# A two-layer transformer block in split fp32: sevens for a second group of k-tiles in half of the gate and up blocks

## The chip, the cores and the metric

One core of one Trainium2 chip. The metric is the device time of one execution in microseconds. Three runs of the kernel before took 2272.69, 2273.01 and 2273.35 us (median 2273.01).

## The reference

The input is one sequence of 256 positions with 2048 features, and two layers. Each layer adds a mixer (gated delta rule and gated linear recurrence in layer 0, two kinds of attention in layer 1) and then a feed-forward part of width 5632:

```python
def swiglu(hn, w_gate, w_up, w_down):
    return (jax.nn.silu(hn @ w_gate) * (hn @ w_up)) @ w_down
...
        h = h + swiglu(rmsnorm(h, ffn_norm[layer]), ffn_w_gate[layer], ffn_w_up[layer], ffn_w_down[layer])
    return rmsnorm(h, final_norm)
```

Everything is fp32. Only the feed-forward parts are changed here.

## The kernel before

**Split products.** TensorE multiplies in the type fp32r. Each fp32 number is taken as a high part (a cast to fp32r, on ACT) and a low part (the number less its high part, on DVE), and a product is the sum of three: high by high, high by low, low by high. `load` (L161) draws a weight tile of 128 x 1024 (512 KB) into a raw buffer, through SP's queue; `split` (L171) makes its parts `whi` (L174, ACT) and `wlo` (L175, DVE). Raw buffers: three in a pool, and in the feed-forward part a fourth, `raw4`, for each fourth load. High parts have four buffers, low parts three.

**The feed-forward part** (`ffn`, L444) runs over 11 columns of 512 hidden features (b = 0 to 10), in pieces of 4, 4 and 3. For each column one block computes gate and up: the four results are F[t][i], t for the two halves of the positions, i for gate or up. Then, per piece, two blocks (p = 0, 1) multiply the hidden features with the down weights, and add to h. The activations (`X` or `hid`) are the stationary operand, 128 x 128; the weights stream, 512 columns for each matmul.

**A block** (`block`, L371) has 16 units of weights (12 in the down blocks of the last piece): a unit is two k-tiles of one of the two weight matrices. Four units, that is four k-tiles of both, form a group m. A plain unit is one load, one cast, one subtraction and 12 matmuls (two halves t, two k-tiles, three products). The group m = 0 is done by sevens instead (Strassen's method in Winograd's form, on the 2 x 2 of halves of positions and k-tiles, and of k-tiles and matrices): 7 products of 6 matmuls in place of 8. It needs sums of weights (`total`, L334: an addition on DVE into T, a cast `thi` on ACT, a subtraction `tlo` on DVE), T1 to T4, and combinations of the activations, made once for a whole layer (X) or piece (hid) by `combine` (L344). Its seven steps, with the loads that they draw:

| step | load | into |
|---|---|---|
| 1 | b11 | M0, b11 itself |
| 2 | b12 | M1, T1 = b11 + b12 |
| 3 | b22 | F01, b22 itself |
| 4 | | M3, T3 = b12 + b22 |
| 5 | | M2, T2 = T1 + b22 |
| 6 | b21 | F00, b21 itself |
| 7 | | F10, T4 = T2 + b21 |

(In the kernel the signs are in the combinations and in the last sums.) After the last step `ends` (L411) makes four sums e of the M banks (one copy on ACT, four steps on DVE), and at the block's end F and e are added.

**The order of the work.** The program writes the units in order, and between the plain units the steps by sevens: step k is written behind plain unit j as soon as k < (j - lead + 2) x steps / gaps (L437). With 12 plain units, lead 2 and trail 3, gaps is 7, so one step follows each of the plain units 1 to 7 (counted from 0), and four plain units stand behind the last one. In the first block of a layer the lead is 5 and the gaps 4: seven steps within four plain units. The framework then schedules each engine's queue, which stays in that order on the chip; a tile waits until one of its tag's buffers is free.

**Hooks** are written ahead of a plain unit: `turn` (L449, twice, ahead of units 2 and 3) transposes the block before's result `fa` on TensorE into a bank Ph and writes its parts into `hid`; `combine` of X in the first block, of the first four hid tiles in the second block of a piece. PSUM has eight banks: four for F, and four that M and Ph share.

Of the kernel before, what the change touches and what calls it, by code (L numbers as in the profile page):

```python
# [4 lines left out]
F32, F32R, I32 = dt.float32, dt.float32r, dt.int32  # L5
# [6 lines left out]
T = 256  # L12
# [35 lines left out]
def body(tc, A, out):  # L48
# [9 lines left out]
    wh = pool("wh", 4)  # L58
    wl = pool("wl", 3)
    acc = pool("acc", 4, space=PSUM)  # L60
    msp = pool("msp", 4, space=PSUM)
    mx, ogp = Phase(), Phase()
    loads, more = [0], []
# [16 lines left out]
    X = res.tile([128, NK, 2, T], F32R, name="X", tag="X")  # L80
# [88 lines left out]
        return raw  # L169

    def split(raw):  # L171
        hi = wh.tile([128, 1024], F32R, name="whi")
        lo = wl.tile([128, 1024], F32R, name="wlo")
        S.copy(hi, raw)  # L174
        V.tensor_sub(lo, raw, hi.bitcast(F32))  # L175
        return hi, lo
# [100 lines left out]

    def sumsq(g, *ts):
        for t in ts or range(2):
            j = mx.tile([128, 512], F32, name="junk", tag="t2", bufs=4)  # L280
            S.activation(j, h[:, t, g * 512:(g + 1) * 512], AF.Square, accum_out=ssp[:, t, g:g + 1])

    def to_x(g, w, late=False):
# [59 lines left out]

    def combine(x4):  # L344

        f = mx.tile([128, 4, T], F32, name="cf", tag="cf", bufs=1)
        c = mx.tile([128, 4, 2, 128], F32, name="cc4", tag="cc4", bufs=1)
        r = mx.tile([128, 2, 4, 2, 128], F32R, name="comb", tag="comb", bufs=2)
        V.tensor_tensor(out=f, in0=x4[:, :, 0].bitcast(F32), in1=x4[:, :, 1].bitcast(F32), op=ALU.add)
        a11, a21, a12, a22 = (f[:, 2 * j:2 * j + 2, t * 128:(t + 1) * 128] for j in range(2) for t in range(2))  # L350
        for i, (x, y) in enumerate(((a21, a22), (a21, a11), (a22, c[:, 1]), (a12, c[:, 2]))):
            V.tensor_tensor(out=c[:, i], in0=x, in1=y, op=ALU.subtract)
        S.copy(r[:, 0], c)
        V.tensor_tensor(out=r[:, 1], in0=c, in1=r[:, 0].bitcast(F32), op=ALU.subtract)
        return r
# [15 lines left out]
    def block(src, x, comb, nd, hooks, tail=0, lead=2):  # L371

        plain = [(i, u) for m in range(nd) if m not in comb for u in (2 * m, 2 * m + 1) for i in range(2)]
        n, ns = len(plain) // 2, len(comb)
        F = [[Bank(acc.tile([128, 512], F32, name=f"F{t}{i}", tag="acc"), n + (ns if t * i == 0 else 0)) for i in range(2)]
             for t in range(2)]  # L380
        M = [Bank(ms([128, 512], f"M{j}"), ns) for j in range(4)]

        def xs(k, t):
            return [x(k)[:, j, t * 128:(t + 1) * 128] for j in range(2)]

        def seven(m):
            c = comb[m]()
            cx = lambda i: lambda kk: [c[:, j, i, kk] for j in range(2)]
            q = lambda j, t: lambda kk: xs(4 * m + 2 * j + kk, t)
            b11 = load(src(0, 2 * m))  # L390
            M[0].add(q(0, 0), split(b11))
            yield
            b12 = load(src(1, 2 * m))
            t, w = total(b11, b12, "T1")
            M[1].add(cx(0), w)
            yield
            b22 = load(src(1, 2 * m + 1))
            F[0][1].add(cx(3), split(b22))
            yield
            M[3].add(cx(1), total(b12, b22, "T3")[1])  # L400
            yield
            t, w = total(t, b22, "T2")
            M[2].add(cx(2), w)
            yield
            b21 = load(src(0, 2 * m + 1))
            F[0][0].add(q(1, 0), split(b21))
            yield
            F[1][0].add(q(1, 1), total(t, b21, "T4")[1])
            yield

        def ends():  # L411
            c1, v, w5, w7 = (mx.tile([128, 512], F32, name=f"e{i}", tag=f"e{i}", bufs=1) for i in range(4))
            S.copy(c1, M[0].t)
            for o, a, b, op in ((v, M[2], c1, ALU.subtract), (w5, M[1], v, ALU.add), (v, M[3], v, ALU.add), (w7, M[3], w5, ALU.add)):
                V.tensor_tensor(out=o, in0=a.t, in1=b, op=op)
            return [[c1, w5], [v, w7]]

        sevens = [s for m in comb for s in [seven(m)] for _ in range(7)]
        trail = 3 if nd > 3 else 2
        gaps = max(len(plain) - lead - trail, 1)  # L420
        held, e, k = [], None, 0
        for j, (i, u) in enumerate(plain):
            if j in hooks:
                hooks[j]()
            w = unit(src(i, u))
            held.append((i, u, w))
            if j < len(plain) - tail:
                todo, held = [(*held[0], (0, 1))], []
            elif j < len(plain) - 1:
                continue  # L430
            else:
                todo = [(*y, (t,)) for t in range(2) for y in held]
            for i1, u1, w1, tt in todo:
                for t in tt:
                    F[t][i1].add(lambda kk: xs(2 * u1 + kk, t), w1)
            tick()
            while k < len(sevens) and k < (j - lead + 2) * len(sevens) // gaps:  # L437
                next(sevens[k])
                k += 1
                if k == len(sevens):  # L440
                    e = ends()
        return [[y.t for y in f] for f in F], e

    def ffn(L, then, fin=None):  # L444

        gu, dn = A[f"gu{L}"], A[f"dn{L}"]
        todo, cx, ch = [], {}, {}

        def turn():  # L449
            hid, j, t, a = todo.pop(0)  # L450
            P = ms([128, 4, 128], "Ph")
            for i in range(4):
                PE.transpose(P[:, i], a[:, i * 128:(i + 1) * 128], tb["ident"])  # L453
            d = hid[:, 4 * j:4 * j + 4, :, t * 128:(t + 1) * 128]
            S.copy(d[:, :, 0], P)
            V.tensor_tensor(out=d[:, :, 1], in0=P, in1=d[:, :, 0].bitcast(F32), op=ALU.subtract)

        b = 0
        for piece in (4, 4, 3):
            hid = ogp.tile([128, 16, 2, T], F32R, name="hid", tag="hid")  # L460
            for j in range(piece):
                hooks = {2: turn, 3: turn} if todo else {}
                if b == 0:
                    hooks[4] = lambda: cx.update({0: combine(X[:, 0:4])})
                    hooks[8] = rstd
                if j == 1:
                    hooks[5] = lambda: ch.update({0: combine(hid[:, 0:4])})
                F, e = block(lambda i, u: gu[b, u, i], lambda k: X[:, k], {0: lambda: cx[0]}, 4, hooks, lead=2 if b else 5)
                a = [mx.tile([128, 512], F32, name=f"fa{t}", tag="fa", bufs=4) for t in range(2)]
                for t in range(2):  # L470
                    r = nrm["rs"][:, t:t + 1]
                    V.tensor_tensor(out=a[t], in0=F[t][0], in1=e[t][0], op=(ALU.add, ALU.subtract)[t])
                    S.activation(a[t], a[t], AF.Silu, scale=r)
                for t in range(2):
                    r = nrm["rs"][:, t:t + 1]
                    V.tensor_tensor(out=e[t][1], in0=F[t][1], in1=e[t][1], op=ALU.add)
                    V.scalar_tensor_tensor(out=a[t], in0=e[t][1], scalar=r, in1=a[t], op0=ALU.mult, op1=ALU.mult)
                    todo.append((hid, j, t, a[t]))
                b += 1
            u0 = 2 * (b - piece)  # L480
            for p in range(2):
                end = b == NB and p == 1
                F, e = block(lambda i, u: dn[2 * p + i, u0 + u], lambda k: hid[:, k], {0: lambda: ch[0]}, piece,
                             {2: turn, 3: turn} if todo else {}, 3 if end and fin else 0)
                hs = [[h[:, t, (2 * p + i) * 512:(2 * p + i + 1) * 512] for i in range(2)] for t in range(2)]
                for t in range(2):
                    for i in range(2):
                        V.tensor_tensor(out=e[t][i], in0=hs[t][i], in1=e[t][i], op=ALU.subtract if t > i else ALU.add)
                for t in range(2):
                    for i in range(2):  # L490
                        V.tensor_tensor(out=hs[t][i], in0=F[t][i], in1=e[t][i], op=ALU.add)
                    if end and fin:
                        fin(t)
                if b == NB and not (end and fin):
                    then(2 * p)
                    then(2 * p + 1)
# [674 lines left out]
```

## Time and profile before

| what | value |
|---|---|
| median of three runs | 2273.01 us |
| the profiled execution: its own time | 2272.64 us |
| its span, first to last instruction | 2270.7 us |
| clock granted to TensorE | 0.999 |
| loads of gate and up weights | 352, 512 KB each, median 4.2 us from issue to landing |
| loads of down weights | 176, 512 KB each, 4.1 us |
| read from HBM | 418.22 MB, 185 GB/s over the span |
| low parts (L175) | 744, 1.22 us each |
| high parts (L174) | 744, 1.05 us each |
| sums T (L337) | 136, 1.22 us each |

A row of a group names the line, the engine, the step, what it writes and reads, the count, then the busy time in us, the mean of one in ns, and the idle time of the engine ahead of them with what ended it. A row in order of time has the start, the length, the engine, and in brackets how long its engine had been idle and who released it. A row of waits has the total, the number and the longest. Line numbers are those of the kernel before.

### The profile page before, as it was taken

The numbers are of one execution on the slowest core, as the hardware profiler recorded it, in microseconds if no ns is written. First come the engines' busy times: TensorE is split into PE (matmuls) and PEld (weight loads), VectorE is DVE, ScalarE is ACT, GpSimd is POOL, SyncE is SP. The second block draws the span as 40 slices with busy tenths as digits, with TensorE's granted clock in tenths as the row PEclk, the third lists the DMA queues.
The fourth block names the chain that finished last, engine by engine and source line by source line (L and its number), as shares of the span: only waits on it lengthen the run. The fifth ranks groups of instructions, "written<-read, shape, count | busy, mean of one in ns | idle before, by whom it ended". The sixth has DMA issues, their size and how long they took to land.

```text
span 2270.7 us, 31138 instructions
## 1 busy us (share of the span) xinstructions
PE 2252.9 (99%) x11610; PEld 1901.3 (84%) x11610; DVE 1804.5 (79%) x2655; ACT 1201.8 (53%) x1579; POOL 2.0 (0%) x6
## 2 busy tenths in 40 slices
PE   9999999999999999999999999999999999999998
PEld 8999888878888888888878888888888888888886
DVE  7898676697887887887976658858888888887888
ACT  6765654564554554454644444445554454554554
POOL 0000000000000000000000000000000000000000
PEclk9999999999999999999999999999999999999999
DMA  7444445566666666666555455555666566566564
GB/s 256 151 160 155 140 158 184 179 203 196 194 205 193 195 202 189 200 197 197 191 163 169 153 169 168 166 187 188 195 208 193 190 201 202 184 203 207 183 217 148
DMA packets 118647, 422.35 MB, mean 186 GB/s; under 512 B 13248, under 2 KB 14784, under 8 KB 118368
## 3 DMA queue, kind: packets, MB, share of 16 engines
q1 hardware_dynamic: 118208, 419.84, 58.3%
q8 instruction: 91, 1.49, 0.3%
q14 instruction: 60, 0.49, 0.1%
q10 hardware_dynamic: 288, 0.52, 0.1%
HBM read 418.22 MB, written 2.10 MB: 185 GB/s over the span
## 4 chain that ended last, share of the span: by engine, by line
PE 94%; DVE 2%; DMA 2%; ACT 0%; issue 0%; SPq 0%; DVEq 0%; ACTq 0%
PE F L366 17%; PE F L368 17%; PE F L367 17%; PE Pw L194 7%; PE Pw L199 6%; PE Px L268 5%; PE Px L270 4%; PE Px L269 4%; PE M L367 2%; PE M L368 2%; PE M L366 2%; PE Pw L197 2%; PE Pw L198 2%; DMA raw<-in_gu 1%; PE Ph L453 1%; DVE wlo L175 1%
## 5 line engine op out<-in xcount | busy, mean ns | idle before, releaser
L174 ACT CAST whi<-raw 128x1024 fp32r<-128x1024 f32 x744 | 779.9, 1052 | 899.9 <-PE F L368 375.5
L175 DVE TENSOR_TENSOR wlo<-raw,whi 128x1024 fp32r<-128x1024 f32 x744 | 904.7, 1220 | 324.3 <-PE F L367 122.1
L366 PE MATMUL F<-whi,X 128*128 128x512 f32 x1100 | 431.0, 392 | 0.0
L367 PE MATMUL F<-wlo,X 128*128 128x512 f32 x1100 | 428.4, 389 | 0.0
L368 PE MATMUL F<-whi,X 128*128 128x512 f32 x1100 | 428.1, 389 | 0.0
L199 PE MATMUL Pw<-X,wlo 128*128 128x256 f32 x1104 | 310.5, 281 | 1.1 <-DVE wlo L175 1.1
L368 PEld LDWEIGHTS F<-whi,X 128*128 128x128 f32 x1100 | 206.5, 188 | 43.1
L367 PEld LDWEIGHTS F<-wlo,X 128*128 128x128 f32 x1100 | 206.6, 188 | 42.1 <-DVE wlo L175 0.5
L366 PEld LDWEIGHTS F<-whi,X 128*128 128x128 f32 x1100 | 206.5, 188 | 41.8
L194 PE MATMUL Pw<-X,whi 128*128 128x512 f32 x640 | 230.3, 403 | 0.0
L199 PEld LDWEIGHTS Pw<-X,wlo 128*128 128x128 f32 x1104 | 209.5, 190 | 1.7 <-DVE wlo L175 1.5
L366 PE MATMUL F<-whi,hid 128*128 128x512 f32 x536 | 209.8, 392 | 0.0
L367 PE MATMUL F<-wlo,hid 128*128 128x512 f32 x536 | 208.7, 389 | 0.0
L368 PE MATMUL F<-whi,hid 128*128 128x512 f32 x536 | 208.7, 389 | 0.0
L341 DVE TENSOR_TENSOR tlo<-T,thi 128x1024 fp32r<-128x1024 f32 x136 | 165.7, 1219 | 24.0 <-ACT thi L340 24.0
L340 ACT CAST thi<-T 128x1024 fp32r<-128x1024 f32 x136 | 142.8, 1050 | 38.0 <-DVE T L337 34.9
L194 PEld LDWEIGHTS Pw<-X,whi 128*128 128x128 f32 x640 | 120.2, 188 | 29.4 <-issue 0.7
L197 PE MATMUL Pw<-X,whi 128*128 128x256 f32 x464 | 135.2, 291 | 0.6 <-ACT whi L174 0.6
L198 PE MATMUL Pw<-X,whi 128*128 128x256 f32 x464 | 131.2, 283 | 0.0
L368 PEld LDWEIGHTS F<-whi,hid 128*128 128x128 f32 x536 | 100.6, 188 | 21.0
L367 PEld LDWEIGHTS F<-wlo,hid 128*128 128x128 f32 x536 | 100.7, 188 | 20.8 <-DVE wlo L175 0.3
L366 PEld LDWEIGHTS F<-whi,hid 128*128 128x128 f32 x536 | 100.6, 188 | 20.3
(371 smaller groups left out, 3229.8 us busy)
## 6 DMA issues: line engine op xcount, KB each, us to landing
raw<-in_gu SPq DMA_DIRECT2D x352, 512.0 KB, 4.2
raw<-in_dn SPq DMA_DIRECT2D x176, 512.0 KB, 4.1
raw<-in_w0w SPq DMA_DIRECT2D x74, 512.0 KB, 3.7
raw<-in_wo SPq DMA_DIRECT2D x64, 512.0 KB, 3.6
raw<-in_w1w SPq DMA_DIRECT2D x64, 512.0 KB, 3.6
raw<-in_w1x SPq DMA_DIRECT2D x32, 512.0 KB, 3.6
raw<-in_w0x SPq DMA_DIRECT2D x16, 512.0 KB, 3.5
raw<-in_w0w SPq DMA_DIRECT2D x12, 256.0 KB, 4.6
```

The costliest lines, as they stand in the source:

```text
L174: S.copy(hi, raw)
L175: V.tensor_sub(lo, raw, hi.bitcast(F32))
L194: PE.matmul(P.rearrange("p a b -> p (a b)"), hi[:, kk], X[:, k].rearrange("p a b -> p (a b)"), start=k == 0, stop=False)
L197: PE.matmul(P[:, 0], hi[:, kk], X[:, k, 0], start=k == 0, stop=False)
L198: PE.matmul(P[:, 0], hi[:, kk], X[:, k, 1], start=False, stop=False)
L199: PE.matmul(P[:, 0], lo[:, kk], X[:, k, 0], start=False, stop=k == NK - 1)
L268: PE.matmul(Ps[t], x[:, 0, ts], hi[:, kk], start=k == 0, stop=False)
L340: S.copy(hi, t)
L341: V.tensor_sub(lo, t, hi.bitcast(F32))
L366: PE.matmul(self.t, xh, hi[:, kk], start=self.i == kk == 0, stop=False)
L367: PE.matmul(self.t, xh, lo[:, kk], start=False, stop=False)
L368: PE.matmul(self.t, xl, hi[:, kk], start=False, stop=kk == 1 and self.i == self.n - 1)
```

## The change

- In every second gate and up block (b = 2, 4, 6, 8, 10 of both layers) the group m = 1 is done by sevens as well: 8 plain units, 14 steps. Each group draws its seven steps from its own generator, first all of m = 0, then all of m = 1. The M banks take both groups. The trail there is 2, so gaps is 4, and the 14 steps stand behind plain units 1 (three), 2 (four), 3 (three) and 4 (four); three plain units follow.
- The combination of X for m = 1 is made in block b = 1, ahead of plain unit 8. That of hid moves from the second to the fourth block of a piece of four. `combine` has three result buffers, and takes its two others from the three buffers of T.
- In the feed-forward part each fifth load's high part, and the low part of each load whose number leaves 2 when divided by 4, gets a buffer of its own.
- `junk` and `fa` have two buffers instead of four.

```diff
     def split(raw):
-        hi = wh.tile([128, 1024], F32R, name="whi")
-        lo = wl.tile([128, 1024], F32R, name="wlo")
+        k = loads[0] if more else 0
+        hi = mx.tile([128, 1024], F32R, name="whi", tag="hi5", bufs=1) if k > 0 and k % 5 == 0 else wh.tile([128, 1024], F32R, name="whi")
+        lo = mx.tile([128, 1024], F32R, name="wlo", tag="lo4", bufs=1) if k > 0 and k % 4 == 2 else wl.tile([128, 1024], F32R, name="wlo")
...
-            j = mx.tile([128, 512], F32, name="junk", tag="t2", bufs=4)
+            j = mx.tile([128, 512], F32, name="junk", tag="t2", bufs=2 if more else 4)
...
-        f = mx.tile([128, 4, T], F32, name="cf", tag="cf", bufs=1)
-        c = mx.tile([128, 4, 2, 128], F32, name="cc4", tag="cc4", bufs=1)
-        r = mx.tile([128, 2, 4, 2, 128], F32R, name="comb", tag="comb", bufs=2)
+        f = mx.tile([128, 4, T], F32, name="cf", tag="T", bufs=3)
+        c = mx.tile([128, 4, 2, 128], F32, name="cc4", tag="T", bufs=3)
+        r = mx.tile([128, 2, 4, 2, 128], F32R, name="comb", tag="comb", bufs=3)
...
-        sevens = [s for m in comb for s in [seven(m)] for _ in range(7)]
-        trail = 3 if nd > 3 else 2
+        two = [seven(m) for m in comb]
+        sevens = [two[i] for i in ((0,) * 7 if ns == 1 else (0,) * 7 + (1,) * 7)]
+        trail = 3 if ns == 1 and nd > 3 else 2
...
-                if j == 1:
+                if j == (3 if piece == 4 else 1):
                     hooks[5] = lambda: ch.update({0: combine(hid[:, 0:4])})
-                F, e = block(lambda i, u: gu[b, u, i], lambda k: X[:, k], {0: lambda: cx[0]}, 4, hooks, lead=2 if b else 5)
-                a = [mx.tile([128, 512], F32, name=f"fa{t}", tag="fa", bufs=4) for t in range(2)]
+                if b == 1:
+                    hooks[8] = lambda: cx.update({1: combine(X[:, 4:8])})
+                F, e = block(lambda i, u: gu[b, u, i], lambda k: X[:, k],
+                             {m: lambda m=m: cx[m] for m in range(2 - b % 2 if b else 1)}, 4, hooks, lead=2 if b else 5)
+                a = [mx.tile([128, 512], F32, name=f"fa{t}", tag="fa", bufs=2) for t in range(2)]
```

## The prediction

> **What bounds the kernel now.** I read the page's first part, then the waits of TensorE, then a feed-forward block in order of time. All microseconds are of one profiled execution: its time is 2272.64, its span 2270.7, so 1.94 lie around the span.
>
> ```profile
> span 2270.7 us, 31138 instructions
> PE 2252.9 (99%) x11610; PEld 1901.3 (84%) x11610; DVE 1804.5 (79%) x2655; ACT 1201.8 (53%) x1579; POOL 2.0 (0%) x6
> ```
> ```profile
> PE Pz L90 <- ACT wz L87: 2.3, 1, 2.3
> PE M L367 <- DVE tlo L341: 1.7, 4, 0.5
> PE Pw L199 <- DVE wlo L175: 1.1, 2, 0.8
> PE Prb L311 <- PE Pw L199: 0.8, 1, 0.8
> PE Pw L197 <- ACT whi L174: 0.6, 1, 0.6
> ```
> TensorE is busy 99% and all its listed waits add to 6.5 us. VectorE (DVE) waits for TensorE, not the other way. So time goes with the number of matmuls, as long as nothing else becomes late. The price of one, from the first and the last of 79 matmuls in a row:
>
> ```profile
> 595.78 0.39 PE L368 MATMUL F<-whi,X 128*128 128x512 f32 x1
> ...
> 613.47 0.39 PE L368 MATMUL F<-whi,X 128*128 128x512 f32 x1
> ```
> 17.69 / 78 = 0.2268 us from start to start. (The 0.39 is the pipelined length of one.) A gate and up block with one group by sevens has 186 such matmuls; its length is the distance of the same step in two neighbouring blocks, 566.73 - 523.65 = 43.08 us:
>
> ```profile
> 523.65 0.69 DVE L472 TENSOR_TENSOR fa<-F,e 128x512 f32<-128x512 f32 x1 [0.31 <-PE F L368]
> ...
> 566.73 0.69 DVE L472 TENSOR_TENSOR fa<-F,e 128x512 f32<-128x512 f32 x1 [0.31 <-PE F L368]
> ```
> 186 x 0.2268 = 42.18; the other 0.90 are the two turns (transposes of fa), 0.45 each. VectorE in this block:
>
> ```profile
> 527.70:570.20 42.50, 42.50 (x193) 35.19 (x193) 34.14 (x35) 22.16 (x24) 0.00 (x0) 1.00 0.62 195
> ```
> The columns are length, PE, PEld, DVE, ACT, POOL, clock, DMA share, GB/s. DVE works 34.1 of 42.5 us, ACT 22.2, the clock is full. Its steps:
>
> ```profile
> 531.37 1.22 DVE L175 TENSOR_TENSOR wlo<-raw,whi 128x1024 fp32r<-128x1024 f32 x1
> 532.51 1.22 DVE L341 TENSOR_TENSOR tlo<-T,thi 128x1024 fp32r<-128x1024 f32 x1
> 533.64 1.21 DVE L175 TENSOR_TENSOR wlo<-raw,whi 128x1024 fp32r<-128x1024 f32 x1
> ...
> 548.82 1.23 DVE L341 TENSOR_TENSOR tlo<-T,thi 128x1024 fp32r<-128x1024 f32 x1 [0.85 <-ACT thi L340]
> ...
> 551.77 2.74 DVE L415 TENSOR_TENSOR e<-M,e 128x512 f32<-128x512 f32 x4 [0.36 <-PE M L368]
> ```
> ```profile
> 558.37 0.39 PE L366 MATMUL F<-thi,X 128*128 128x512 f32 x1
> ```
> A step of 1024 columns comes every 1.14 us, one of 512 about every 0.62 to 0.68. The last low part of the group (T4) is done at 550.05 and first needed at 558.6: 8 us in hand.
>
> **What the change removes.** Ten blocks change: every second gate and up block (the third, fifth, ... eleventh) of two layers. Their second group of four k-tiles gets 7 products instead of 8; a product is 6 matmuls. The instruction order of the two builds says the same: 10529 rows on TensorE instead of 10589. 60 x 0.2268 = **13.6 us** less, 1.36 in a block (43.08 to 41.72).
>
> **What it adds on ACT and DVE.** Four plain units (a cast and a subtraction each) give way to 3 split weights and 4 totals: per block 3 casts more on ACT (3 x 1.05, to some 25 of 41.7 us: no bound) and on DVE 7 low parts + 4 additions - 4 = 7 steps more. DVE: 34.1 + 7 x 1.14 = **42.1 us against 41.7** for TensorE. That is the crux: in these blocks DVE has no slack over the whole block, and lives on what it did ahead. The block after it (34.1 against 43.1) lets it recover.
>
> The loads stay 16 per block, but each group's are drawn together. The steps by sevens now run 3 or 4 behind each plain unit, and all 14 lie behind plain units 2 to 5. SP's queue issues a load when its raw buffer is free, and there are four. So I followed DVE's queue of the built kernel from the block's first matmul (t = 0), with the steps above. In a block with turns, DVE may read F10 of the block before at -2.72 + 0.30 (the 0.31 above); then come 13 steps up to the addition T4 of the first group (fa, b11, e, T3, fa, e, b22, fa, T3's low part, T2, j2, b21, T4): 8 x 1.14 + 3 x 0.62 + 2 x 0.68 = 12.34, end at t = 9.9. That addition frees the raw buffer of the second group's b22, and ACT's queue has the cast of that b22 **ahead of** the cast of T4. So T4's low part stands behind an addition, a load, two casts and a subtraction. The kernel before has such a chain once in a layer, in its first block, where 7 steps are packed into 4 plain units:
>
> ```profile
> 454.03 1.14 DVE T L337
> 455.20 4.34 DMA raw<-in_gu
> 459.62 1.06 ACT whi L174
> 460.71 1.24 DVE wlo L175
> 461.96 3.50 DMA raw<-in_gu
> 465.55 0.47 DVE T L337
> 466.02 0.68 issue
> 466.69 1.23 DVE tlo L341
> 467.97 0.50 PE M L367
> ```
> ```profile
> 458.90 0.50 PE L367 MATMUL M<-tlo,comb 128*128 128x512 f32 x1 [0.33 <-DVE tlo L341]
> ...
> 467.97 0.50 PE L367 MATMUL M<-tlo,comb 128*128 128x512 f32 x1 [0.47 <-DVE tlo L341]
> ```
> ```profile
> L340 ACT CAST thi<-T 128x1024 fp32r<-128x1024 f32 x136 | 142.8, 1050 | 38.0 <-DVE T L337 34.9 <-PE M L368 2.2 <-DVE wlo L175 0.3
> ```
> With its prices: load and its gaps 4.45, cast 1.06, cast 1.05, subtraction 1.22: 7.8 us. T4's low part is there at 17.7. TensorE wants it after 75 matmuls and a turn: 17.0 + 0.45 = 17.5. 0.2 late. Then seven steps of 1.14 (T1's low part, b22, T2, T3's low part, j4, b21, T4 of the second group) end at 25.7; ACT again has the cast of a load that this T4 frees (the next block's first unit) ahead of T4's cast: 25.7 + 7.8 = 33.5. TensorE wants it after 139 matmuls and two turns, at 32.4: **1.1 us late** in all, the 0.2 included. Six blocks are so. In the four that come behind a down projection no turn lies in the block and the queue is shorter: T4 at 8.2, low part at 15.9 (wanted at 17.0), second one at 8.0 + 7.8 later, 31.7, wanted at 31.5: 0.2 late. Together 6 x 1.1 + 4 x 0.2 = **7.4 us**, 0.74 a block; the nearest row that measures it is the first block above: 0.33 + 0.47 = 0.8 us of waits. Bounds: 0 (loads a bit faster) and 3.0 a block (below).
>
> **What I cost at nothing.** The extra buffers (one high part for each fifth load, one low part for each fourth) only let DVE and ACT go ahead; the most that they can win is TensorE's wait for low parts in feed-forward, 1.7 us above. The one more combination per layer and the moved ones lie in blocks with one group:
>
> ```profile
> L354 DVE TENSOR_TENSOR comb<-cc,comb 128x1024 fp32r<-128x1024 f32 x8 | 9.7, 1217 | 0.0
> L349 DVE TENSOR_TENSOR cf<-hid 128x1024 f32<-128x1024 f32 x6 | 7.3, 1225 | 0.2
> L352 DVE TENSOR_TENSOR cc<-cf 128x256 f32<-128x256 f32 x16 | 6.0, 418 | 0.0
> L352 DVE TENSOR_TENSOR cc<-cf,cc 128x256 f32<-128x256 f32 x16 | 6.7, 417 | 0.0
> ```
> 1.22 + 1.22 + 4 x 0.42 = 4.1 us of DVE: 34.1 + 4.1 = 38.2 of 43.1, hidden by the matmuls; without that cover two more would cost 8.2. That cf and cc now share three buffers with the totals delays T2 behind them, by less than the 8 us in hand. Fewer fa and junk buffers: fa is turned early in the next block; junk is written by ACT alone, in order. Three plain units instead of four behind the last step leave 8.2 us for the four e steps (2.74 above).
>
> By "Perfetto Trace Analysis" of the Trainium skill, section Identifying the Most-Contended Engine, matmul busy time is a bad measure of how near TensorE is to its limit, and the busy share of weight loads a better one. Here that share is 84%, near DVE's 79%, so by it the 60 matmuls could be worth 0.84 x 13.6 = 11.4 us, or nothing if something else set the pace. The rows speak against the second: the distance of 0.2268 holds over 79 matmuls with no wait between them.
>
> **Sum.** 2272.64 - 13.6 + 7.4 = **2266.4**. The profiled execution lies 0.4 under the median of the three runs (2273.01); I leave that in the range.
>
> **Rivals.**
> 1. *Chains hidden.* If loads land as the 3.50 above rather than 4.34, both chains are 0.84 shorter and T4 comes in time in all blocks: 2272.64 - 13.6 = 2259.0. For it: the median below is 3.9. Against: three loads follow each other within 3.4 us here.
>
> ```profile
> DMA to landing us min/median/max: 2.6/3.9/8.4
> ```
> 2. *Loads eat it.* Each load slower by d delays the second T4 by 2d. At d = 0.3 the loss is 0.74 + 0.6 = 1.34 a block, which is the whole gain: 2272.4. For it: maximum 8.4 and 4.34 with fewer loads at once. Against: the load of b22 is the last of three, and its predecessors are under way.
> 3. *VectorE becomes the bound, slower than before.* In the blocks with one group DVE loses time inside the sevens:
>
> ```profile
> L341 DVE TENSOR_TENSOR tlo<-T,thi 128x1024 fp32r<-128x1024 f32 x68 | 82.8, 1219 | 10.5 <-ACT thi L340 10.5
> L337 DVE TENSOR_TENSOR T<-T,raw 128x1024 f32<-128x1024 f32 x34 | 41.5, 1220 | 6.0 <-DMA raw<-in_gu 4.6 <-DMA raw<-in_dn 1.4
> L337 DVE TENSOR_TENSOR T<-raw 128x1024 f32<-128x1024 f32 x34 | 41.4, 1216 | 1.3 <-DMA raw<-in_gu 1.2
> ```
> (one layer, 17 groups): 17.8 / 17 = 1.05 us a group. Two groups: 42.1 + 2.1 = 44.2 against 41.7, 2.5 a block; with half a microsecond for waits on buffers, 3.0. If nothing of it is absorbed: 2272.64 - 13.6 + 30 = 2289. It decides from 1.36 a block, and from 1.8 it can be told from no change. Against: 8 us in hand at the end of a group, and the last low part is wanted 9.3 us (41 matmuls) before the block ends.
> 4. *Matmuls removed buy nothing* (the rule above): 2272.6 or more.
>
> **How the numbers follow.** Forecast (0.3 to 0.9 lost a block) 0.38; rival 1, 0.20; rival 2, 0.22; rival 3, 0.18; rival 4, 0.02. A measurement of this kernel tells about 0.2% (4.5 us, a loss under 0.9 a block) from no change. Faster: 0.38 + 0.20 = 0.58; same: 0.22 + 0.02 = 0.24; slower: 0.18. Low end: all hidden and the 1.7 us of waits gone as well, 2257.4. High end: 2.2 lost a block, 2281, which leaves out the worse part of rival 3.
>
> **What would show it.** TensorE rows fewer by 60; waits of TensorE for tlo, and at T4 above all, 0 to 1 us twice in each of ten blocks; distance between the fa steps around a changed block 42 to 43 us instead of 43.08; DVE near 100% there; odd blocks unchanged at 43.1. Wrong if TensorE waits for wlo too, if it waits at F banks (fa late) or for Ph's bank (behind ACT's copy of M0), or if odd blocks grow.

## The result and the profile after

The changed kernel takes **2281.45 us** (median of 6 runs, 2279.73 to 2283.00) against 2272.63 for the kernel before (6 runs beside it, 2270.96 to 2273.35): a ratio of 1.0039, 95% interval 1.0026 to 1.0052. It is slower, by 0.4%. The forecast was 2266.4; the time lies 0.4 us above the high end of the range.

The first lines of the page of the kernel after:

```profile
span 2277.9 us, 31039 instructions
PE 2255.6 (99%) x11550; PEld 1889.4 (83%) x11550; DVE 1887.3 (83%) x2737; ACT 1228.9 (54%) x1611; POOL 2.0 (0%) x6
```
The 60 matmuls are gone (11610 to 11550), and yet TensorE's busy time is 2.7 us *longer* than before (2252.9). Waits alone do not make busy time grow while matmuls go: some matmuls seem to take longer. So I looked at two things, waits and the distance from one matmul to the next. The waits of TensorE's matmuls, kernel after:

```profile
PE F L368 <- DVE tlo L342: 4.9, 13, 0.8
...
PE M L367 <- ACT thi L341: 1.4, 2, 0.9
```
F waits for tlo, which it didn't before: a matmul into F that streams tlo is the step T4. Now the distances. The same 168 rows in a row without a wait, in the kernel before and then in the kernel after, first and last in order of time: they go from the second turn of the column b = 3, which the change leaves alone, to the first turn of the block behind it.

```profile
582.63 0.39 PE L367 MATMUL F<-wlo,X 128*128 128x512 f32 x1
...
620.50 0.27 PE L453 MATMUL Ph<-tab,fa 128*128 128x128 f32 x1
```
```profile
582.82 0.39 PE L368 MATMUL F<-wlo,X 128*128 128x512 f32 x1
...
621.02 0.28 PE L455 MATMUL Ph<-tab,fa 128*128 128x128 f32 x1
```
37.87 / 167 = 226.8 ns before, 38.20 / 167 = 228.7 after, both at full clock, with nothing waiting in between. Matmuls have become dearer in a block whose steps are those of before.

All feed-forward matmuls together, worked out from their starts in the trace (us; a distance under 0.3 counts as a matmul's price, the rest above 0.2268 as a wait; "waits" are those between matmuls and those ahead of a turn, and include a distance of some 0.32 next to each turn that both kernels have; 6132 and 6072 matmuls make 6131 and 6071 distances, since nothing follows the last one):

| kernel | span | matmuls x 0.2268 | dearer distances | waits |
|---|---|---|---|---|
| before | 2270.7 | 1390.5 | 0.5 | 9.0 |
| after | 2277.9 | 1376.9 | 10.5 | 20.7 |
| difference | +7.2 | -13.6 | **+10.0** | **+11.7** |

(The remaining -0.9 lies outside these distances; the stretch behind the last matmul alone is 1.2 us shorter.) Of the 11.7 us of waits, 11.4 lie in the ten changed blocks. And where the time of whole blocks lies, from the first matmul of a block to the first of the next, summed over ten blocks of each kind, with three of the experiments below (runs 5, 7 and 11):

| ten blocks | before | after | high_aligned | aligned_spread | raw5_only |
|---|---|---|---|---|---|
| with a second group by sevens | 427.1 | 428.4 | 433.0 | 428.6 | 416.3 |
| gate and up with one group (b = 1, 3, 5, 7, 9) | 430.9 | 436.1 | 434.1 | 435.5 | 432.2 |
| down (without the last of each layer) | 405.8 | 408.4 | 405.6 | 405.6 | 405.6 |

The wait itself, in the chain of waits of the kernel after, around the second changed column (b = 4; the block begins at 700.03):

```profile
707.55 1.15 DVE T L338
708.71 4.97 DMA raw<-in_gu
...
714.73 1.05 ACT thi L341
715.80 1.24 DVE tlo L342
...
725.17 4.88 DMA raw<-in_gu
...
730.14 0.06 ACT whi L175
730.21 0.89 issue
731.10 1.05 ACT thi L341
732.17 1.24 DVE tlo L342
733.41 0.04 issue
733.46 0.50 PE F L368
```
The addition ahead of the second load, from VectorE's rows of the same stretch:

```profile
723.88 1.22 DVE L338 TENSOR_TENSOR T<-T,raw 128x1024 f32<-128x1024 f32 x1
...
732.17 1.22 DVE L342 TENSOR_TENSOR tlo<-T,thi 128x1024 fp32r<-128x1024 f32 x1 [2.53 <-ACT thi L341]
```
This is the chain that the prediction described, twice in the block: addition T4, a load into the buffer that it frees, the cast of that load, T4's cast behind it on ACT, T4's low part, TensorE. VectorE stands idle for 2.53 us in the middle of it. (The view puts a cast that ended at 725.15 ahead of the second load. The addition ended at 725.10, and the waits of SP's queue between 720 and 730 us name it, with 1.9 us; run 11 bears this out.)

### The profile page after: what moved, and what is told of

It is laid out like the page before. It is cut to its first block, busy times and chain, and to the rows that moved or that the text cites. A ratio compares the mean times of both kernels' runs of the same rounds, so it can differ in the third digit from the quotient of the medians.

```text
span 2277.9 us, 31039 instructions
## 1 busy us (share of the span) xinstructions
PE 2255.6 (99%) x11550; PEld 1889.4 (83%) x11550; DVE 1887.3 (83%) x2737; ACT 1228.9 (54%) x1611; POOL 2.0 (0%) x6
## 4 chain that ended last, share of the span: by engine, by line
PE 86%; DVE 5%; DMA 5%; ACT 2%; issue 1%; SPq 0%; DVEq 0%; ACTq 0%
PE F L368 14%; PE F L369 14%; PE F L367 14%; PE Pw L195 7%; PE Pw L200 6%; PE Px L269 5%; PE Px L270 4%; PE Px L271 4%; DMA raw<-in_gu 4%; PE Pw L198 3%; PE M L368 2%; PE M L367 2%; PE Pw L199 2%; PE M L369 2%; DVE wlo L176 2%
## 5 line engine op out<-in xcount | busy, mean ns | idle before, releaser
L175 ACT CAST whi<-raw 128x1024 fp32r<-128x1024 f32 x734 | 767.5, 1051 | 809.1 <-PE F L369 304.2
L176 DVE TENSOR_TENSOR wlo<-raw,whi 128x1024 fp32r<-128x1024 f32 x734 | 888.3, 1221 | 237.1 <-issue 69.9
L367 PE MATMUL F<-whi,X 128*128 128x512 f32 x960 | 377.5, 393 | 0.0
L368 PE MATMUL F<-wlo,X 128*128 128x512 f32 x960 | 375.8, 392 | 0.0
L369 PE MATMUL F<-whi,X 128*128 128x512 f32 x960 | 374.5, 390 | 0.0
L342 DVE TENSOR_TENSOR tlo<-T,thi 128x1024 fp32r<-128x1024 f32 x176 | 214.7, 1221 | 39.2 <-ACT thi L341 38.8
L341 ACT CAST thi<-T 128x1024 fp32r<-128x1024 f32 x176 | 184.4, 1050 | 106.0 <-DVE T L338 89.3
L369 PEld LDWEIGHTS F<-whi,X 128*128 128x128 f32 x960 | 180.2, 188 | 39.1
L367 PEld LDWEIGHTS F<-whi,X 128*128 128x128 f32 x960 | 180.2, 188 | 38.5
L368 PEld LDWEIGHTS F<-wlo,X 128*128 128x128 f32 x960 | 180.3, 188 | 38.0 <-DVE wlo L176 0.3
```

The costliest lines, as they stand in the source:

```text
L341: S.copy(hi, t)
L342: V.tensor_sub(lo, t, hi.bitcast(F32))
L367: PE.matmul(self.t, xh, hi[:, kk], start=self.i == kk == 0, stop=False)
L368: PE.matmul(self.t, xh, lo[:, kk], start=False, stop=False)
L369: PE.matmul(self.t, xl, hi[:, kk], start=False, stop=kk == 1 and self.i == self.n - 1)
```

## The experiments

Letters in the expectations: **A**, the extra buffers make matmuls dearer (A1: because they lie high in SBUF; A2: because of where they start, counted modulo 256 bytes); **C**, TensorE waits at T4 for the chain through a freed raw buffer. The rivals: VectorE has too much to do (rival 3 of the prediction; **B** in runs 1 and 2, **D** in runs 7 and 8), the number of buffers alone decides (**B** in run 3), and a fifth raw buffer speeds up the loads whatever is computed (**E**). "Dearer distances" and "waits" are the two columns of the table above, from the one profiled execution of each run. Start addresses are those of the built kernels: the usual weight buffers, X, hid and the combinations all start at 192 modulo 256; in the kernel after the extra high and low buffers start at 64, because twelve small tiles of 32 bytes lie ahead of them. Each time stands beside runs of the kernel before on the same chip; diffs are against the kernel after unless another is named.

**1. The change without the extra buffers.**

```diff
-        k = loads[0] if more else 0
-        hi = mx.tile([128, 1024], F32R, name="whi", tag="hi5", bufs=1) if k > 0 and k % 5 == 0 else wh.tile([128, 1024], F32R, name="whi")
-        lo = mx.tile([128, 1024], F32R, name="wlo", tag="lo4", bufs=1) if k > 0 and k % 4 == 2 else wl.tile([128, 1024], F32R, name="wlo")
+        hi = wh.tile([128, 1024], F32R, name="whi")
+        lo = wl.tile([128, 1024], F32R, name="wlo")
```


> The changed kernel without the two added buffers (hi5, lo4); everything else stays. In the changed kernel matmuls that stream from lo4 start the next one after 233 ns and those from hi5 after 231 ns, where the others of before took 226.8 ns; summed over the feed-forward matmuls this is 10.0 us more, and gaps over 300 ns add another 11.8 us. Theory A (the place of the two buffers makes their matmuls slow): the 10 us go, the gaps stay or grow a little for want of buffers: 2271 us (2268 to 2276). Theory B (VectorE is the bound of the ten blocks, the buffers help it): gaps grow, 2285 us or more.

2278.39 us, ratio 1.0021 (1.0011 to 1.0031). The dearer distances fall from 10.5 to 1.7 us, as theory A has it, but the waits grow to 26.4. They move, too: from F to M, the steps T1 to T3. The waits of its weight loads on TensorE:

```profile
PEld M L367 <- DVE tlo L341: 14.1, 20, 1.5
PEld F L367 <- DVE tlo L341: 5.6, 10, 1.0
```
The expected 2271 was missed. Why the waits move to M was not tried apart; their length is not for want of the two buffers alone, since run 5 has both, with matmuls at full speed, and its waits are 29.2.

**2. The extra buffers alone**, with one group by sevens as before (the kernel before, with the two `split` lines, the smaller `fa` and `junk`, and `combine`'s two other results in T's buffers, as in the change).

> The kernel before with the two added buffers alone (and the smaller fa, junk and combination buffers that make room for them); no second group by sevens. Theory A: the matmuls that stream from them get slow as in the changed kernel, 9 to 11 us more than before: 2282 us (2279 to 2285). Theory B: no change or a little faster, 2271 to 2273 us.

2287.49 us, ratio 1.0065 (1.005 to 1.008): the buffers alone cost more than the whole change. Dearer distances 10.6 us, as expected of A; with the waits of 14.2, which A did not foresee, the time is above its 2279 to 2285. The added waits lie in b = 1, 5 and 9 of both layers (1.1 to 1.4 us a column, ahead of matmuls into M), the columns in which the combination of hid is made here. The like stretch of 168, in the column b = 2, whose steps here are those of before:

```profile
542.24 0.39 PE L368 MATMUL F<-wlo,X 128*128 128x512 f32 x1
...
580.39 0.27 PE L454 MATMUL Ph<-tab,fa 128*128 128x128 f32 x1
```
38.15 / 167 = 228.4 ns. Matmuls that stream from the low buffer come 233.4 ns apart, from the high one 230.8, from the others 227 to 228.

**3 and 4. The same buffers lower in SBUF**, allocated ahead of the other tags (start at 192), and once more with 128 bytes of padding ahead of them (start at 64, and with them thi, tlo, T and the combinations).

```diff
+            mx.tile([128, 32], F32, name="pad", tag="pad", bufs=1)        (4 only)
+        for tag, dtype, n in (("hi5", F32R, 1), ("lo4", F32R, 1), ("thi", F32R, 2), ("tlo", F32R, 2)):
+            mx.tile([128, 1024], dtype, name="at", tag=tag, bufs=n)
```


> The changed kernel, same number of buffers, but the two added ones and those of thi and tlo stand first in the feed-forward pool: hi5 at byte 146624 of a partition instead of 220736, lo4 at 150720 instead of 208448. Theory A: starts of matmuls go back to 226.8 ns, 10 us less than the changed kernel: 2271 us (2267 to 2274). Theory B (number of buffers, or that each has a tag of its own): as the changed kernel, 2281 us.

> As the one with low places, with 128 bytes put ahead of them: hi5, lo4, thi and tlo then begin at 64 modulo 256, as hi5 and lo4 did in the changed kernel (the fast buffers begin at 192 modulo 256). Theory A1 (the upper part of SBUF is slow to stream from): as with low places, 2271 us. Theory A2 (the start within 256 bytes decides): all four kinds slow, 2281 to 2290 us.

| | time | ratio | dearer distances | waits |
|---|---|---|---|---|
| 3, start 192 | 2278.96 | 1.0022 (1.0012 to 1.0032) | 1.7 | 29.7 |
| 4, start 64 | 2286.55 | 1.0060 (1.0045 to 1.0075) | 14.8 | 22.2 |

Run 3 misses both its expectations (2271 and 2281): the dear distances go, as A has it, but the waits grow to 29.7. A shift of 128 bytes makes 7.6 us. In run 4 the combinations, which are stationary, start at 64 as well, so pairs can be told apart. Mean distances by the starts of the streamed and the stationary tile: 192 with 192: some 228 ns; 64 with 64: between 228 and 229; 64 with X at 192: 232; 192 with a combination at 64: 232. It is not the place of one tile but whether both start alike. Matmuls with like starts are a little dear too (228 to 229 for 226.8), more so where an unlike pair stands close by (some 229) than elsewhere (228).

**5. High in SBUF, but aligned**: the kernel after with 128 bytes behind the small tiles, so that both extra buffers start at 192. The tiles allocated behind them move by the same 128 bytes; nothing else is changed.

```diff
+        if more:
+            mx.tile([128, 32], F32, name="pad", tag="pad", bufs=1)
```


> The changed kernel, its order and its places, with 128 bytes put behind the small tiles of the feed-forward pool, so that lo4 begins at byte 208576 and hi5 at 220864 of a partition: 192 modulo 256, as the weights' other buffers, X, hid and the combinations. Theory A1 (the upper part of SBUF is slow to stream from): no change, 2281 us. Theory A2 (a matmul is slow when the tile that streams and the tile that is loaded as weights begin at different places modulo 256): starts go back to 227 ns for both, some 9 us less than the changed kernel in pitch; the waits of TensorE for T4 grow as with low places, since they no longer have slow matmuls to hide in: 2275 to 2279 us.

2279.64 us, ratio 1.0025 (1.0015 to 1.0035); dearer distances 2.1 us. The stretch of 168 in b = 3:

```profile
584.92 0.39 PE L370 MATMUL F<-wlo,X 128*128 128x512 f32 x1
...
622.79 0.38 PE L457 MATMUL Ph<-tab,fa 128*128 128x128 f32 x2
```
37.87 / 167 = 226.8, as before the change. That ends A1: the buffers lie as high as in the kernel after. But of the 8.4 us that the matmuls give back little arrives: by the medians some 3 us (5.8 above the kernel before instead of 8.8, and the intervals overlap), in the profiled executions none (spans 2278.9 and 2277.9; the one is the slowest of its nine runs, the other the fastest of its six). The waits grow from 20.7 to 29.2. Waits of its matmuls:

```profile
PE F L370 <- DVE tlo L344: 8.4, 17, 0.8
PE M L369 <- ACT thi L343: 2.3, 2, 1.3
```
So in the kernel after the dear matmuls had hidden some 5 to 8 us of the same stall. At full speed the waits cost 29.2 - 9.0 = 20.2 us more than before the change, 18.3 of them in the ten changed blocks.

**6. What each distance costs** (the kernel before, buffers of high parts padded so that they start 0, 64, 128 and 192 bytes from X modulo 256, low ones 0, 32 and 64; the smaller `fa` makes room).

```diff
+    pool("pad", 1).tile([128, 40], F32, name="pad")
...
-        hi = wh.tile([128, 1024], F32R, name="whi")
-        lo = wl.tile([128, 1024], F32R, name="wlo")
+        hi = wh.tile([128, 1040], F32R, name="whi")[:, 0:1024]
+        lo = wl.tile([128, 1032], F32R, name="wlo")[:, 0:1024]
...
```


> The kernel before (fa with two buffers), whose four buffers for high parts begin 0, 64, 128 and 192 bytes off the place of X modulo 256, and whose three for low parts 0, 32 and 64 bytes off. Theory A2: matmuls that stream from the buffer at 0 start every 227 ns, from the one at 128 every 231 to 234 ns, the others show how the price goes with the distance; the whole is slower than before by 5 to 25 us. Theory A1: all as before, 226.8 ns, 2273 us.

One run, 2304.52 us, dearer distances 28.2. All buffers come out between 230.5 and 232.8 ns, the one at distance 0 among them, where 227 was expected of A2. That unlike neighbours raise the like ones, as in run 4, would fit, but was not tried apart. The price by distance could not be separated; that a mixture of starts costs 4 to 6 ns on every matmul is what this run shows.

**7. The steps spread over five plain units in place of four** (run 5 with trail 1 in the changed blocks).

```diff
-        trail = 3 if ns == 1 and nd > 3 else 2
+        trail = 1 if ns == 2 else 3 if nd > 3 else 2
```


> The one with aligned high places, and trail 1 in the blocks with two groups: the 14 steps lie behind five plain units (2, 3, 3, 3, 3) instead of four, and two plain units follow the last. Theory C (the chain from T4 through the load that it frees back to T4's own cast sets the waits): the second T4 has 2.7 us more, waits of TensorE for tlo halve, 4 to 8 us faster than the aligned one: 2268 to 2273 us. Theory D (VectorE has too much to do in the whole block, wherever the steps lie): waits move to another place and the time stays within 2 us of the aligned one.

2278.58 us, ratio 1.0024 (1.0012 to 1.0036). The waits for T4 are all but gone (0.3 us, at one weight load), and another has come in the six blocks with turns:

```profile
PE Ph L457 <- ACT e L416: 11.5, 6, 2.3
```
The turn's bank Ph is one of the four that M uses, and with the steps later it isn't free until ACT has copied M0; the distance to the turn's first matmul is 2.0 to 2.7 us each time. This is the trade that the prediction named under "Wrong if", not taken by the change itself. By its time, which stays within 2 us of run 5, this run speaks for theory D and against C's 2268 to 2273; the next run has the same work on VectorE and decides between them.

**8. A raw buffer in place of the extra high one** (run 5 without hi5, and with a buffer of its own for each load whose number leaves 2 when divided by 4, the way `raw4` does it).

```diff
+        elif more and loads[0] > 0 and loads[0] % 4 == 2:
+            raw = mx.tile([128, 1024], F32, name="raw5", tag="raw5", bufs=1)
...
-        hi = mx.tile([128, 1024], F32R, name="whi", tag="hi5", bufs=1) if k > 0 and k % 5 == 0 else wh.tile([128, 1024], F32R, name="whi")
+        hi = wh.tile([128, 1024], F32R, name="whi")
```


> The one with aligned high places, with a fifth raw buffer (each load whose number leaves 2 when divided by 4) in place of the extra buffer for high parts. Theory C: the load of the second group's b22 and of the next block's first unit no longer wait for T4, so T4's cast is not late behind theirs: waits of TensorE for tlo fall from some 13 to under 5 us, 6 to 12 us faster than the aligned one: 2265 to 2272 us. Theory D: no faster than the aligned one by more than 2 us.

**2262.82 us, ratio 0.9948 (0.9932 to 0.9965)**: faster than both kernels, and below the 2265 to 2272 expected. Waits 12.2 us (9.0 before), dearer distances 1.8. With five raw buffers the load behind T4 no longer needs the buffer that T4 frees, and VectorE, with the same work, keeps up.

**9. The control: run 8 with one group by sevens as before**, that is the kernel before with the raw buffer and the aligned low one (and the smaller `junk`, `fa` and shared T buffers that make room).

> The kernel before (one group by sevens in every block) with the fifth raw buffer and the aligned low buffer of the last run. Theory C (the buffer helps only because it cuts the chain from T4 through a freed raw buffer, which the kernel before doesn't have): all its waits for low parts in feed-forward are some 2 us, so 2272 us, within 0.15% of before. Rival E (a fifth raw buffer speeds up the loads whatever is computed, and the second sevens give nothing): some 2262 to 2265 us.

2274.08 us, ratio 1.000 (0.9991 to 1.001); waits 9.5, dearer distances 1.2. The raw buffer gives nothing by itself: the gain of run 8 is that of the 60 matmuls, once the chain is cut.

**10. Run 8 without the 128 bytes** (its low buffer starts at 64 again).

> The last run's kernel without the 128 bytes of padding: its extra low buffer starts 64 bytes above a multiple of 256 while the stationary tiles start at 192. Theory A2 (the price hangs on where the streamed tile starts against the stationary one, modulo 256): 116 units x 4 matmuls x 6.4 ns = 3 us in that buffer, and half as much again in its neighbours, excess of the distances 1.8 to about 6 us, time 2265 to 2268. If the starts don't matter: 2263 us. The raw buffer's own start, moved as well, matters to nothing on TensorE.

2265.63 us, ratio 0.9967 (0.9954 to 0.998); dearer distances 5.4 us in place of 1.8, with only 116 of the 484 low parts of feed-forward weights in that buffer. As expected by A2.

**11. Run 8 without the extra low buffer**: the change with one raw buffer in place of its two.

> The last run's kernel without the extra low buffer, so the change plus one raw buffer alone. Theory C: the raw buffer is what was missing, and the low one adds little: 2262 to 2266 us, waits for low parts under 10 us. Rival (low parts stand in each other's way, as the longer waits of the kernel without extra buffers, 2278 us, suggest): 2268 us or more, with M waiting for tlo again by some 20 us.

**2263.18 us, ratio 0.9952 (0.9935 to 0.9968)**, as run 8. Its page, and the longest of its matmuls' waits:

```profile
span 2263.5 us, 31107 instructions
PE 2243.7 (99%) x11550; PEld 1890.1 (84%) x11550; DVE 1884.6 (83%) x2737; ACT 1235.2 (55%) x1611; POOL 2.0 (0%) x6
```
```profile
PE M L372 <- DVE tlo L346: 2.7, 5, 1.0
```
F's wait for tlo is gone. The second T4 of the same column as in the chain above (this block begins at 701.46), in order of time:

```profile
727.39 1.22 DVE L342 TENSOR_TENSOR T<-T,raw 128x1024 f32<-128x1024 f32 x1
...
729.05 1.05 ACT L177 CAST whi<-raw 128x1024 fp32r<-128x1024 f32 x1 [1.16 <-DMA raw<-in_gu]
...
730.38 1.05 ACT L345 CAST thi<-T 128x1024 fp32r<-128x1024 f32 x1 [0.27 <-PE M L373]
...
731.46 1.22 DVE L346 TENSOR_TENSOR tlo<-T,thi 128x1024 fp32r<-128x1024 f32 x1 [0.59 <-ACT thi L345]
...
733.08 0.39 PE L372 MATMUL F<-tlo,X 128*128 128x512 f32 x1
```
From the end of T4's addition to the end of its low part: 732.68 - 728.61 = 4.1 us, against 733.40 - 725.10 = 8.3 in the kernel after. The cast of a load is still ahead of T4's cast, but that load was under way already. T4 is ready 0.4 us ahead of its matmul, though its addition ends later in the block (27.2 us from the block's start against 25.1).

## Why the prediction was wrong

Two steps failed, both with more time than the forecast gave them.

**The first step that failed**, in the prediction's own words: the extra buffers "only let DVE and ACT go ahead; the most that they can win is TensorE's wait for low parts in feed-forward, 1.7 us above". They were costed by what they give VectorE and ACT, and nothing was set for what they do to TensorE, which reads them. They start at 64 modulo 256 where all that they are multiplied with starts at 192, and the matmuls of feed-forward took **10.0 us** more; that the starts do it is shown by runs 3 and 4, 5, and 8 and 10. No row of the profile before could show this price, since every buffer there starts alike; the addresses of the built kernel could have raised the question, and the range had no term for it.

**The second: the stall, right in its place and too small.** "Together 6 x 1.1 + 4 x 0.2 = 7.4 us" against 11.4 in the ten changed blocks of the kernel after, and 18.3 there with matmuls at full speed (run 5). Of the two this one decides the time: without the dear distances the kernel is still 0.25% slower than before (run 5), without the stall it is 0.5% faster (runs 8 and 11). The mechanism was as described, in all ten blocks, and run 11 settles it by cutting the load out of the chain. Its size was off at both ends. In the column shown, the chain measures 8.3 where the prediction had 7.8, its load taking 4.88 and not 4.34; and the second T4 addition ends 25.1 us after the block's start where the prediction had 15.9 + 8.0 = 23.9, since the first chain was late as well (low part at 717.03 - 700.03 = 17.0, not 15.9). Rival 2 had priced this: each load slower by d costs 2d, as each T4 passes its delay on.

**The removal** was right: 60 matmuls, 13.6 us, and run 11 against run 9 gives 2274.08 - 2263.18 = 10.9 of it by the medians. In their profiled executions (9.0 apart in the span) waits take 2.1 us more (11.6 against 9.5) and distances 0.7; the rest was not traced.

**The sum.** Forecast -13.6 + 7.4 = -6.2; measured in the span -13.6 + 11.7 + 10.0 - 0.9 = +7.2, and +8.8 in the medians.

**The rivals.** Rival 3 had the right side. It named the time that VectorE loses inside the sevens while it waits for thi, which the rows below confirm, but its mechanism, VectorE's total as the bound of the block, is not what happened. One row by stage for the fifth changed column, of the kernel after and of run 11 (length, PE, PEld, DVE, ACT):

```profile
1044.87:1088.14 43.27, 42.70 (x190) 34.27 (x189) 41.01 (x43) 25.23 (x28) 0.00 (x0) 1.00 0.62 195
```
```profile
1040.95:1082.82 41.87, 41.87 (x190) 34.49 (x189) 41.60 (x43) 25.37 (x28) 0.00 (x0) 1.00 0.64 201
```
VectorE is busy 99% of the block in the *fast* kernel, and TensorE waits for nothing there; in the slow one VectorE has 2.3 us idle. The forecast's "42.1 us against 41.7" was thus a fair count that by itself costs nothing there. In the kernel after VectorE lost time inside the sevens, waiting for ACT, which waited for a load. The low parts of totals, kernel after and run 11 (busy, mean, idle ahead of them):

```profile
L342 DVE TENSOR_TENSOR tlo<-T,thi 128x1024 fp32r<-128x1024 f32 x176 | 214.7, 1221 | 39.2 <-ACT thi L341 38.8
```
```profile
L346 DVE TENSOR_TENSOR tlo<-T,thi 128x1024 fp32r<-128x1024 f32 x176 | 214.6, 1220 | 23.7 <-ACT thi L345 23.2
```
Rival 1 (2259.0, loads as short as 3.50) didn't come by itself; run 11 comes to 2263.2 by another way. Rival 4 (the removed matmuls buy nothing) is out: in run 11 they bring 10.9 us.

**"Odd blocks unchanged at 43.1"** was wrong as well: 43.6 on average. 0.35 of each is the price of the matmuls (43.4 in most of them); the rest lies in b = 9 (44.1 and 44.6), where M waits for thi behind the combination of hid. Runs 1 and 5, without the fifth raw buffer, have this wait too (1.5 to 1.7 us), in runs 8 and 11, with it, 0.2 to 0.4 us are left, and in run 11 b = 9 takes 43.4. Why the same combination costs nothing in b = 3 and 7 was not tried.

**What stays open:** what in the chip makes unlike starts dear, and the price by distance (run 6 could not tell). Apart from run 6 only starts of 64 and 192 occur, so whether the period is 256 bytes, or another that keeps these two apart, was not tried either.

## What to carry to other kernels

A buffer that is added for one engine is also an operand of another: before costing it at nothing, look where it starts against the tiles that it is multiplied with, and where the profile shows busy time growing while instructions fall, compare distances from start to start in a stretch without waits. When a chain runs through a load, the buffer to add is the one that the load waits for (here a raw one: the change without extra buffers is at +0.2%, with the raw one added at -0.5%), not those of the results behind it (run 5, +0.25%). And a stall measured next to slower work can be too small: speed the work up, and the stall may take the time back.

## What the runs showed of the hardware

**Starts of the two operands.** With the streamed and the stationary tile both at the same start modulo 256 bytes, a 128 x 128 by 512 fp32r matmul follows the one before it after 226.8 ns; with 128 bytes between the starts after 231 to 234, and neighbours lose 1 to 2 ns. Moving the same buffers by 128 bytes switches it (runs 3 and 4, 8 and 10). The Trainium skill, "SBUF — State Buffer", section "Who interferes with whom", gives TensorE one read port for the streamed operand and an independent one for weight loads, and says that it never waits on anyone. That is said of the engines among each other and names no start addresses; what these runs show of them is not in it.

**The clock after a wait.** In run 7, after the longest wait at the turn's bank, matmuls came at half speed: the granted clock was 0.51 from 2183 to 2186 us, and 0.997 over the whole run.

```profile
2181.34 0.66 PE L457 MATMUL Ph<-tab,fa 128*128 128x128 f32 x4 [2.35 <-ACT e L416]
...
2182.94 0.63 PE L371 MATMUL F<-whi,X 128*128 128x512 f32 x1
...
2185.50 0.60 PE L371 MATMUL M<-thi,comb 128*128 128x512 f32 x1
```
2.56 us for six distances, 427 ns each. No other stretch of its feed-forward part came at that distance, though five more such waits, of 2.0 to 2.65 us from start to start, lie in it (this one: 2.73). The Trainium skill, "TensorE: Matmul & The Clock Gate", section "Wait — 56ns, not 53.3ns?", gives 426.7 ns as the distance at half clock, which these rows agree with. The Trainium skill, "TensorE: Matmul & The Clock Gate", section "What's actually happening", has the clock fall after an idle window of about 3.4 us. Here, in the one case seen, it fell after 2.35 us of idleness.
